# A decoder trunk in float32 pairs: four of eleven pairs of gate and up by seven products instead of eight

## The chip, the cores and the metric

The kernel runs on one core of one Trainium2 chip. The metric is the device time of one execution in microseconds (us). The engines are TensorE (PE, with its weight loads as PEld), VectorE (DVE), ScalarE (ACT), GpSimd (POOL) and SyncE (SP); transfers are issued from the queues of SP and Pool and carried by 16 DMA engines.

## The reference

Two decoder layers over x of 512 positions and 1024 features, float32. Each layer adds a token mixer and then a SwiGLU feed-forward part, each followed by a layer norm:

```python
def _swiglu(x, w_gate, w_up, w_down):
    return (jax.nn.silu(x @ w_gate) * (x @ w_up)) @ w_down

def reference(x, ...):
    for i in range(DEPTH):                       # DEPTH = 2
        h = _multiscale_pool(...) if i % 2 == 0 else _diff_attention(...)
        x = _layernorm(ALPHA * x + h, ln_mix_g[i], ln_mix_b[i])
        x = _layernorm(ALPHA * x + _swiglu(x, w_gate[i], w_up[i], w_down[i]), ln_ffn_g[i], ln_ffn_b[i])
    return x
```

The hidden width is 2816, that is 22 blocks of 128. Layer 0 mixes by pooling, layer 1 by attention.

## The kernel before

**Numbers.** Every float32 factor of a product is split into a high part (cast to the format that TensorE takes, on ACT) and a low part (value minus high part, on DVE). A product is three matmuls: high x high, high x low, low x high (`mm3`, lines 106 to 110).

**Weights.** All weights lie in one array `wall` of chunks of 128 x 1024. `fetch` loads a chunk from SP's queue into one of four buffers `raw`; `ready` casts it into `wh` (line 89) and makes `wl` (line 90), six buffers each.

**The feed-forward part, gate and up.** `ffn(layer, late)` treats the 22 blocks in the order 0, 11, 1, 12, and so on, so that block k and block k + 11 make pair k. For each block f, `product` runs 8 x 3 matmuls for gate and as many for up, with the weights stationary and x (`xt`, kept in two halves of 256 positions, high and low) moving, 512 columns at once. `gated` takes silu on ACT (line 459) and multiplies on DVE into `hid` (line 460). The first blocks (`early`: three in layer 0, two in layer 1) run first for the lower 256 positions and then for the upper 256, since x of the upper half comes late.

**The down product by seven products.** The product of `hid` with `w_down` is done by Strassen's scheme in Winograd's form: seven half-size products P1, Q5, P6, Q3, P7, P2, Q4 in place of eight. Its sums are made during gate and up. `sum_weights(k)` (lines 474 to 486) loads four blocks of the down weights from SP's queue (line 482), makes four sums on DVE (line 484) and stores them from Pool's queue into `tsum` in device memory (line 486); it runs eleven times a layer. `sum_hidden(k)` (lines 491 to 511) makes the sums of pair k of `hid`, keeps the high and low part of one quarter in `a11`, and stores the others, `v`, to `ssum` from Pool's queue (line 509). `items` is the list of down products; `prepare`, `split_item` and `left` get the factors of the next ones ready.

**Order.** Each engine and each queue carries out its instructions in the order in which the program issues them; the order is written out by hand, there is no planner. An instruction that waits holds what stands behind it on its engine or queue. `affine` (lines 188 ff.) applies a norm's scale and shift to `res`, two operations on DVE for each of four blocks of positions; before, it is called after the blocks that follow the early ones.

Of the kernel before, what the change touches and what calls it, by code (L numbers as in the profile page):

```python
# [12 lines left out]
F32 = mybir.dt.float32  # L13
# [32 lines left out]
DOWN = ("P1", "Q5", "P6", "Q3", "P7", "P2", "Q4")  # L46
PAIRS = [(0, 2), (2, 2), (4, 2), (6, 2), (8, 2), (10, 1)]
# [3 lines left out]
def trunk(ctx, tc, x, wall, pscale, lam_p, subln, table, lng, lnb, band, first, onehot, out):  # L51
# [85 lines left out]
    def load_gb(n):  # L137
        gb = keep.tile([P, 2, D], F32, tag="gb", name=f"gb{n}")
        nc.sync.dma_start(out=gb[:, 0, :], in_=lng[n : n + 1, :].broadcast_to([P, D]))
        nc.sync.dma_start(out=gb[:, 1, :], in_=lnb[n : n + 1, :].broadcast_to([P, D]))  # L140
        gbs[n] = gb
# [291 lines left out]

    ROWS = [slice(k, k + n) for k, n in PAIRS]

    def ffn(layer, late):
        n = 2 * layer + 1
        final = n == 2 * DEPTH - 1
        c0 = base[0]
        with tc.tile_pool(name=f"ffn{layer}", bufs=1) as fp:  # L440
# [5 lines left out]
            def product(acc, c, lo, hi):  # L446
                h, l = weights(c)
                for k in range(KB):
                    mm3(
                        wide(acc, lo, hi),  # L450
                        (h[:, k * P : (k + 1) * P], l[:, k * P : (k + 1) * P]),
                        x_at(k, lo, hi),
                        k == 0,
                        k == KB - 1,
                    )

            def gated(f, pg, pu):
                sg = keep.tile([P, S], F32, tag="y", name=f"sg{layer}_{f}", bufs=2)
                nc.scalar.activation(sg, pg, AF.Silu)  # L459
                nc.vector.tensor_tensor(hid[:, f, :], sg, pu, op=ALU.mult)  # L460

            c1 = c0 + 2 * FB
# [11 lines left out]
            def sum_weights(k):  # L474

                i, j = k // 2, k % 2
                c = slice(j * 512, (j + 1) * 512)
                b11, b12, b21, b22 = t = [
                    fp.tile([P, 512], F32, tag=f"b{b}", name=f"b{b}_{layer}_{k}") for b in range(4)
                ]  # L480
                for b in range(4):
                    nc.sync.dma_start(out=t[b], in_=block(i, b)[:, c])
                for z, x, y in ((b11, b11, b12), (b12, b12, b22), (b22, b11, b22), (b21, b22, b21)):
                    nc.vector.tensor_tensor(z, x, y, op=ALU.add)  # L484
                for m, z in enumerate((b11, b22, b12, b21)):
                    nc.gpsimd.dma_start(out=tsum[m, i, :, c], in_=z)

            late_low = []
            summed_rows = [0]

            def sum_hidden(k):
                first, second = hid[:, k, :256], hid[:, k, 256:]
                a12, a22 = hid[:, k + HALF, :256], hid[:, k + HALF, 256:]
                u = fp.tile([P, 2, 256], F32, tag="u", name=f"u{layer}_{k}", bufs=1)
                v = fp.tile([P, 2, 2, 256], F32R, tag="v", name=f"v{layer}_{k}", bufs=1)
                tt = nc.vector.tensor_tensor
                nc.scalar.copy(a11[:, 0, k, :], first)
                tt(second, second, a22, op=ALU.subtract)
                tt(a11[:, 1, k, :], first, a11[:, 0, k, :].bitcast(F32), op=ALU.subtract)
                tt(first, second, first, op=ALU.subtract)  # L500
                nc.vector.scalar_tensor_tensor(
                    u[:, 0, :], first, -1.0, a22, op0=ALU.mult, op1=ALU.subtract
                )
                tt(u[:, 1, :], a12, first, op=ALU.add)
                nc.scalar.copy(v[:, :, 0, :], u)  # L505

                def rest():
                    tt(v[:, :, 1, :], u, v[:, :, 0, :].bitcast(F32), op=ALU.subtract)
# [8 lines left out]
            early = 3 if layer == 0 else 2  # L517
            accs = [(bank(f"g{layer}_{f}"), bank(f"u{layer}_{f}")) for f in range(early)]
            for lo in (0, 256):
                for f in range(early):  # L520
                    for i in range(2):
                        product(accs[f][i], c0 + 2 * f + i, lo, lo + 256)
                        if not lo and (f, i) in late:
                            late[f, i]()
                        if not lo:
                            ready(c0 + 2 * early)
                    if lo:
                        ready(c0 + 2 * f + 6)
                        gated(order[f], *accs[f])
            sum_hidden(0)  # L530
            if layer:
                load_gb(n - 1)
# [570 lines left out]
```

## Time and profile before

| | |
|---|---|
| median of 3 runs | 981.76 us (979.96 to 982.25) |
| profiled execution | 983.17 us, its span 981.1 us |
| granted TensorE clock, mean | 0.995 |
| busy share: PE, DVE, ACT, POOL | 98%, 66%, 43%, 13% |
| moved by DMA | 188.59 MB, 192 GB/s in the mean |

The span runs from the first to the last instruction of the profiled execution. Busy times are unions of instruction spans, which for PE include the drain of one matmul under the next; the distance between the starts of two matmuls tells what one costs. In the rows of groups the count stands behind x, then the busy time and the mean of one in ns, then the idle time of the engine just before them and what ended it. In the rows of stretches the columns are the length, then each engine's busy time with its count, the granted clock, the share of the DMA engines and GB/s.

### The profile page before, as it was taken

The numbers are of one execution on the slowest core, as the hardware profiler recorded it, in microseconds if no ns is written. First come the engines' busy times: TensorE is split into PE (matmuls) and PEld (weight loads), VectorE is DVE, ScalarE is ACT, GpSimd is POOL, SyncE is SP. The second block draws the span as 40 slices with busy tenths as digits, with TensorE's granted clock in tenths as the row PEclk, the third lists the DMA queues.
The fourth block names the chain that finished last, engine by engine and source line by source line (L and its number), as shares of the span: only waits on it lengthen the run. The fifth ranks groups of instructions, "written<-read, shape, count | busy, mean of one in ns | idle before, by whom it ended". The sixth has DMA issues, their size and how long they took to land.

```text
span 981.1 us, 13416 instructions
## 1 busy us (share of the span) xinstructions
PE 963.2 (98%) x4974; PEld 820.6 (84%) x4974; DVE 643.4 (66%) x1007; ACT 420.5 (43%) x708; POOL 123.7 (13%) x195
## 2 busy tenths in 40 slices
PE   8999999999999999999999999999999999999995
PEld 8898888888888888988888888988888888888884
DVE  6845874455567577688777676756655555477687
ACT  5753222223326357656556554732223322244460
POOL 4201111111120211000000000011111111111102
PEclk9999999999999999999999999999999999999997
DMA  8247768655776984323222122276665566878942
GB/s 223 66 158 247 250 228 289 229 193 193 266 257 236 329 295 151 114 82 94 73 87 86 55 86 86 90 270 211 225 256 193 209 229 228 288 246 297 341 145 86
DMA packets 70079, 188.59 MB, mean 192 GB/s; under 512 B 15956, under 2 KB 16084, under 8 KB 70014
## 3 DMA queue, kind: packets, MB, share of 16 engines
q1 hardware_dynamic: 56588, 141.57, 42.1%
q0 software_dynamic: 13408, 46.15, 13.9%
q8 instruction: 39, 0.64, 0.3%
q14 instruction: 26, 0.21, 0.1%
q10 hardware_dynamic: 18, 0.02, 0.0%
HBM read 150.99 MB, written 36.72 MB: 191 GB/s over the span
## 4 chain that ended last, share of the span: by engine, by line
PE 94%; DVE 3%; ACT 1%; POOL 1%; issue 0%; POOLq 0%; DVEq 0%
PE P L629 13%; PE g L109 8%; PE u L108 8%; PE u L109 8%; PE g L108 8%; PE u L110 8%; PE g L110 8%; PE Q L629 6%; PE s L814 2%; PE v L108 2%; PE v L110 2%; PE v L109 2%; PE wo L108 2%; PE wo L109 2%; PE wo L110 2%; PE q L109 1%
## 5 line engine op out<-in xcount | busy, mean ns | idle before, releaser
L90 DVE TENSOR_TENSOR wl<-raw,wh 128x1024 fp32r<-128x1024 f32 x118 | 141.7, 1220 | 33.3 <-ACT wh L89 33.3
L89 ACT CAST wh<-raw 128x1024 fp32r<-128x1024 f32 x120 | 123.5, 1050 | 65.9 <-PE u L109 63.9
L109 PE MATMUL g<-xt,wh 128*128 128x512 f32 (+1 forms) x392 | 144.1, 368 | 0.5 <-DVE xt L90 0.5
L108 PE MATMUL g<-xt,wh 128*128 128x512 f32 (+1 forms) x392 | 144.3, 368 | 0.0
L108 PE MATMUL u<-xt,wh 128*128 128x512 f32 (+1 forms) x392 | 144.1, 368 | 0.0
L110 PE MATMUL u<-xt,wl 128*128 128x512 f32 (+1 forms) x392 | 144.0, 367 | 0.0
L109 PE MATMUL u<-xt,wh 128*128 128x512 f32 (+1 forms) x392 | 144.0, 367 | 0.0
L110 PE MATMUL g<-xt,wl 128*128 128x512 f32 (+1 forms) x392 | 144.0, 367 | 0.0
L460 DVE TENSOR_TENSOR hid<-sg,u 128x512 f32<-128x512 f32 x44 | 30.3, 688 | 154.9 <-PE u L110 154.5
L90 DVE TENSOR_TENSOR dl<-r,dh 128x1024 fp32r<-128x1024 f32 x84 | 94.3, 1132 | 38.8 <-ACT dh L89 38.7
L89 ACT CAST dh<-r 128x1024 fp32r<-128x1024 f32 x84 | 81.5, 979 | 69.6 <-PE P L629 31.7
L629 PE MATMUL P<-dh,xt 128*128 128x512 f32 x352 | 109.4, 390 | 0.0
L109 PEld LDWEIGHTS g<-xt,wh 128*128 128x128 f32 x392 | 73.9, 189 | 12.7 <-DVE xt L90 0.7
L110 PEld LDWEIGHTS u<-xt,wl 128*128 128x128 f32 x392 | 73.9, 189 | 12.3
L108 PEld LDWEIGHTS u<-xt,wh 128*128 128x128 f32 x392 | 73.9, 189 | 12.1
L110 PEld LDWEIGHTS g<-xt,wl 128*128 128x128 f32 x392 | 73.9, 188 | 12.2
L108 PEld LDWEIGHTS g<-xt,wh 128*128 128x128 f32 x392 | 73.9, 188 | 12.2
L109 PEld LDWEIGHTS u<-xt,wh 128*128 128x128 f32 x392 | 73.9, 188 | 12.0
L505 ACT CAST v<-u 128x512 fp32r<-128x512 f32 x22 | 13.7, 621 | 159.4 <-issue 142.5
L629 PEld LDWEIGHTS P<-dh,xt 128*128 128x128 f32 x352 | 66.1, 188 | 13.6
L484 DVE TENSOR_TENSOR b<-b,b 128x512 f32<-128x512 f32 x88 | 60.8, 691 | 18.4 <-DMA b<-in_wall 16.2
L459 ACT ACTIVATE sg<-g 128x512 f32<-128x512 f32 x44 | 26.3, 599 | 103.5 <-PE g L110 102.0
(189 smaller groups left out, 1792.5 us busy)
## 6 DMA issues: line engine op xcount, KB each, us to landing
raw<-in_wall SPq DMA_DIRECT2D x128, 512.0 KB, 4.2
b<-in_wall SPq DMA_DIRECT2D x88, 256.0 KB, 5.6
tsum<-b POOLq DMA_DIRECT2D x88, 256.0 KB, 4.7
r<-tsum SPq DMA_DIRECT2D x40, 512.0 KB, 4.7
r<-in_wall SPq DMA_DIRECT2D x30, 512.0 KB, 5.0
ssum<-v POOLq DMA_DIRECT2D x22, 512.0 KB, 4.0
xt<-ssum POOLq DMA_DIRECT2D x20, 512.0 KB, 6.0
res<-in_x SPq DMA_DIRECT2D x8, 256.0 KB, 6.4
```

The costliest lines, as they stand in the source:

```text
L89: nc.scalar.copy(dst_h, src)
L90: (low or nc.vector).tensor_tensor(dst_l, src, dst_h.bitcast(F32), op=ALU.subtract)
L108: nc.tensor.matmul(acc, ah, bh, start=start, stop=False)
L109: nc.tensor.matmul(acc, ah, bl, start=False, stop=False)
L110: nc.tensor.matmul(acc, al, bh, start=False, stop=stop)
L459: nc.scalar.activation(sg, pg, AF.Silu)
L460: nc.vector.tensor_tensor(hid[:, f, :], sg, pu, op=ALU.mult)
L484: nc.vector.tensor_tensor(z, x, y, op=ALU.add)
L505: nc.scalar.copy(v[:, :, 0, :], u)
L629: nc.tensor.matmul(accs[s], x[:, k, r], y[:, c], start=first and k == 0 and e == 0, stop=last and k == m - 1 and e == 2, skip_group_check= ...
L814: nc.tensor.matmul(accs[c][:, :wide], a[r, qs], b[r, :wide], start=i == 0, stop=i == 2)
```

## The change

**Split pairs.** Pairs 3, 5, 7 and 9 (`SPLIT`) of gate and up are done by the same seven products (`strassen`). The two-by-two blocks are the two halves of x's features against the two halves of positions, and gate and up of the pair. Each of the seven products is 2 x 4 x 3 matmuls of 256 columns, into three banks A, C and B. P1, P6, P7 and Q4 add up in A, Q5 and Q3 in C; after P1, Q5 and P6 ACT copies the bank out before the next product adds to it, after Q3, P7 and P2 DVE combines it with what was copied, and silu and the products of `gated` follow. The seven products need seven weight chunks made from four loaded ones: four sums on DVE (`sum` in `steps`).

**Sums of x.** `sums_of_x` makes the four sums of quarters of x that these products need, with their high and low parts, into `xs`, in steps between the products of the first blocks. `xs` later holds the left factors of the down product, in place of parts of `xt` and of `a11`, which is gone: P1's factors are split in `left`, and `left` makes P6's difference.

**Order of casts.** In `steps`, a chunk's cast comes ahead of the low part of the chunk before it. `advance` works these steps off; `refill` loads ahead as buffers come free.

**Down sums.** `load_terms(k + 1)` is issued a slot ahead of its use, from Pool's queue: four plain loads and, when the first two have landed, two loads that add to what is there (`accum_op`). `sum_terms(k)` makes the other two sums on DVE and stores all four. The buffers are rows of `hid` that are not yet in use, or the tile `gb`. For row 2 the sums stand ahead of the next load, since both use the same rows.

**Moved.** `affine` runs with blocks 0 to 3, three of them in the early stage of layer 0; the loads of `gb` are moved, in layer 1 to Pool's queue.

The diff, cut to its core:

```diff
+SPLIT = (3, 5, 7, 9)
+GATE = ("P1", "Q5", "P6", "Q3", "P7", "P2", "Q4")
...
-            a11 = fp.tile([P, 2, HALF, 256], F32R, name=f"a11_{layer}")
+            xs = fp.tile([P, 4, 2, 4, 256], F32R, name=f"xs{layer}")
...
+            def step(kind, j):
+                if kind == "cast" and steps and steps[-1][0] == "low":
+                    steps.insert(len(steps) - 1, (kind, j))
+                else:
+                    steps.append((kind, j))
...
+                    chunks += [(c, ()), (c, (c, c + 1)), (c, (c, c + 2)), (c + 2, ())]
+                    chunks += [(c + 1, (c + 1, c + 2)), (c + 3, ()), (c, (c, c + 3))]
+                    step("cast", j0)
+                    for w in (
+                        "low 0, sum 1, cast 1, sum 4, cast 3, cast 4, low 1, sum 2, cast 2, low 3, "
+                        "low 2, sum 6, cast 5, cast 6, low 4, low 5, low 6"
+                    ).split(", "):
+                        steps.append((w[:-2], j0 + int(w[-1])))
...
+            def load_terms(k):
+                ...
+                for q, b in enumerate((0, 1, 3, 2)):
+                    nc.gpsimd.dma_start(out=t[q], in_=block(i, b)[:, c])
+                for q, b in ((0, 1), (1, 3)):
+                    nc.gpsimd.dma_start(out=t[q], in_=block(i, b)[:, c], accum_op=ALU.add)
+                terms[k] = t
+
+            def sum_terms(k):
+                ...
+                t1, t3, b22, b21 = terms.pop(k)
+                tt(b22, t1, b22, op=ALU.add)                                   # line 648
+                tt(b21, b22, b21, op=ALU.add)
+                for m, z in enumerate((t1, b22, t3, b21)):
+                    nc.gpsimd.dma_start(out=tsum[m, i, :, c], in_=z)
+
+            def weight_sums():
+                k = summed_rows[0]
+                summed_rows[0] += 1
+                if k == 2:
+                    sum_terms(k)
+                if k + 1 < HALF:
+                    load_terms(k + 1)
+                if k != 2:
+                    sum_terms(k)
...
             def sum_hidden(k):
...
-                nc.scalar.copy(a11[:, 0, k, :], first)
-                tt(second, second, a22, op=ALU.subtract)
-                tt(a11[:, 1, k, :], first, a11[:, 0, k, :].bitcast(F32), op=ALU.subtract)
-                tt(first, second, first, op=ALU.subtract)
...
+                tt(u[:, 0, :], first, second, op=ALU.subtract)
+                tt(second, second, a22, op=ALU.subtract)
+                tt(u[:, 1, :], a12, first, op=ALU.subtract)
+                tt(u[:, 1, :], u[:, 1, :], second, op=ALU.add)
                 nc.scalar.copy(v[:, :, 0, :], u)
...
+            for lo in (0, 256):
+                for f in range(early):
+                    for i in range(2):
+                        product(accs[f][i], 2 * f + i, lo, lo + 256)
...
+                    if lo:
+                        advance(2 * f + 6)
+                        gated(order[f], *accs[f])
+                        affine(n - 1, f)
+                        weight_sums()
+                        if f < 2:
+                            next(sums)
+            sum_hidden(0)
...
+            def plain(f):
...
+                for i in range(2):
+                    product(a[i], j + i, 0, S)
+                    ahead(j + i + 5)
+                    if f >= 3:
+                        next(sums, None)
+                    if i == 0:
+                        settle()
+                gated(order[f], *a)
+                if f < SB:
+                    affine(n - 1, f)
+                if f in (2, 5, 8, 9, 12, 13, 16, 17, 20):
+                    weight_sums()
+                if f % 2:
+                    sum_hidden(k)
+
+            def strassen(k):
+                names = {"P1": "A", "P6": "A", "P7": "A", "Q4": "A", "Q5": "C", "Q3": "C", "P2": "B"}
...
+                for j, p in enumerate(GATE):
+                    acc = banks[names[p]]
+                    h, l = halves[index[k] + j]
+                    xh, xl = lefts[p]
+                    for f in range(2):
+                        o = acc[:, f * 256 : (f + 1) * 256]
+                        for kk in range(4):
+                            c = slice((4 * f + kk) * P, (4 * f + kk + 1) * P)
+                            for e, (w, x) in enumerate(((h, xh), (h, xl), (l, xh))):
+                                nc.tensor.matmul(o, w[:, c], x[:, kk, :], ...)      # line 794
+                    acc = both(acc)
+                    if p == "P1":
+                        g0 = tile_of(0)
+                        nc.scalar.copy(both(g0), acc)                            # line 803
+                    elif p == "Q5":
+                        nc.scalar.copy(second, acc)                              # line 805
+                    elif p == "P6":
+                        nc.scalar.copy(first, acc)                               # line 807
+                    elif p == "Q3":
+                        tt(first, acc, first, op=ALU.subtract)
+                    elif p == "P7":
+                        tt(second, second, acc, op=ALU.subtract)
+                    elif p == "P2":
+                        tt(both(g0), acc, both(g0), op=ALU.add)
+                        nc.scalar.activation(g0, g0, AF.Silu)
+                    else:
+                        g1 = tile_of(1)
+                        nc.scalar.activation(both(g1), acc, AF.Silu)
+                    ahead(index[k] + j + 6)
+                    if p == "P1":
+                        settle()
+                    elif p == "P2":
+                        tt(first, both(g0), first, op=ALU.mult)
+                    elif p == "Q4":
+                        tt(second, both(g1), second, op=ALU.mult)
+                sum_hidden(k)
```

More of the change, by code (lines that the diff above doesn't have):

```diff
@@ L476, in sum_weights @@
+            terms = {}
+            def load_terms(k):
                 i, j = k // 2, k % 2
                 c = slice(j * 512, (j + 1) * 512)
[L478 to L484, printed above, removed]
@@ L577, in prepare @@
                 while prepared[0] < min(upto, len(items)):
[L578 to L580 removed]
+                    refill()
                     split_item(prepared[0])
+                    held[0] -= 1
                     prepared[0] += 1
@@ L608, in ffn @@
+            f = early
+            while f < FB:
+                if f // 2 in SPLIT:
+                    strassen(f // 2)
+                    f += 2
+                else:
+                    plain(f)
+                    f += 1
+            load_gb(n)
             settle()
```

258 lines of the change are left out of this document (179 added, 79 removed).

## The prediction

> **What bounds the kernel now.** I read the page's busy shares first, then the chain that ended last, then the busy time by stage, then the timeline where the change acts.
>
> ```profile
> span 981.1 us, 13416 instructions
> ## 1 busy us (share of the span) xinstructions
> PE 963.2 (98%) x4974; PEld 820.6 (84%) x4974; DVE 643.4 (66%) x1007; ACT 420.5 (43%) x708; POOL 123.7 (13%) x195
> ...
> PE 94%; DVE 3%; ACT 1%; POOL 1%; issue 0%; POOLq 0%; DVEq 0%
> ```
>
> TensorE is busy for 98% of the span and carries 94% of the chain. A busy PE is no proof of a full PE, so the stages of layer 0 come next: the start of gate and up, the rest of it, and the down product.
>
> ```profile
> core 0: us, PE busy (x) PEld busy (x) DVE busy (x) ACT busy (x) POOL busy (x), PEclk, DMA share, GB/s
> 40.90:77.35 36.45, 36.44 (x304) 36.44 (x305) 18.02 (x22) 20.87 (x37) 2.24 (x4) 1.00 0.41 136
> 77.35:284.10 206.75, 206.75 (x913) 171.17 (x913) 119.91 (x168) 57.39 (x77) 29.35 (x52) 1.00 0.70 241
> 284.10:382.60 98.50, 98.50 (x435) 81.04 (x434) 73.48 (x94) 50.65 (x65) 13.38 (x20) 1.00 0.75 264
> ```
>
> In all three PE has no gap. So only less PE work can gain, and anything that makes PE wait is a loss at its full length. DVE has room: 18 of 36 us, 120 of 207, 73 of 98.5.
>
> **What PE saves.** A plain pair of gate and up (four chunks) issues 4 x 8 x 3 = 96 matmuls of 512 columns; a split pair issues 7 x 2 x 4 x 3 = 168 of 256 columns. The price is the step from one start to the next. The chain view gives 512 columns, PE's timeline in the half-width start of the same stage gives 256:
>
> ```profile
> 77.35 0.23 PE g L108
> ...
> 88.25 0.23 PE g L108
> ```
>
> ```profile
> 59.91 0.28 PE L108 MATMUL g<-xt,wh 128*128 128x256 f32 x1
> ...
> 62.78 0.28 PE L108 MATMUL u<-xt,wh 128*128 128x256 f32 x1
> ```
>
> 48 matmuls in 10.90 us are 0.2271 each, 24 in 2.87 us are 0.1196 each. So the half-width one costs 53%, not 50%, of a wide one. Plain: 96 x 0.2271 = 21.80 us. Split: 168 x 0.1196 = 20.09 us. The saving is 1.71 us a pair, not an eighth of 21.8 (2.7), and 13.7 us for eight pairs (four in each of two layers). That is the ceiling of the change.
>
> The Trainium skill ("TensorE: Matmul & The Clock Gate", Back-to-back issue gap) gives the isolated gap as N/2.4 + 2.5 ns, 215.8 and 109.2 for these widths; by it the saving would be 2.4 us a pair, 19 us in all. The rows above differ from it, and they decide.
>
> **What DVE and ACT get.** Prices of the pieces, on their engines:
>
> ```profile
> L90 DVE TENSOR_TENSOR wl<-raw,wh 128x1024 fp32r<-128x1024 f32 x118 | 141.7, 1220 | 33.3 <-ACT wh L89 33.3
> L89 ACT CAST wh<-raw 128x1024 fp32r<-128x1024 f32 x120 | 123.5, 1050 | 65.9 <-PE u L109 63.9 <-issue 1.3 <-ACT line L422 0.7
> ```
>
> ```profile
> 197.88 0.42 DVE L498 TENSOR_TENSOR hid<-hid 128x256 f32<-128x256 f32 x1
> 198.22 0.42 DVE L499 TENSOR_TENSOR a<-hid,a 128x256 fp32r<-128x256 f32 x1
> 198.68 0.42 DVE L500 TENSOR_TENSOR hid<-hid 128x256 f32<-128x256 f32 x1
> ...
> 201.58 1.22 DVE L90 TENSOR_TENSOR wl<-raw,wh 128x1024 fp32r<-128x1024 f32 x1 [1.68 <-ACT wh L89]
> 202.72 0.69 DVE L508 TENSOR_TENSOR v<-u,v 128x512 fp32r<-128x512 f32 x1
> 203.32 2.87 DVE L484 TENSOR_TENSOR b<-b,b 128x512 f32<-128x512 f32 x4
> 206.10 1.22 DVE L90 TENSOR_TENSOR wl<-raw,wh 128x1024 fp32r<-128x1024 f32 x1
> ```
>
> ```profile
> 102.44 1.22 DVE L189 TENSOR_TENSOR res<-res,gb 128x1024 f32<-128x1024 f32 x1
> ...
> 103.69 1.23 DVE L190 TENSOR_TENSOR res<-res,gb 128x1024 f32<-128x1024 f32 x1
> ```
>
> From start to start a 1024-wide operation costs 1.14 us when the next is independent and 1.25 when it depends; 512-wide 0.60 and 0.70; 256-wide 0.34 and 0.46.
>
> Steady state (a split pair and the plain pair beside it, 20.1 + 21.8 = 41.9 us of PE): 11 low parts and 4 weight sums, 15 x 1.14 = 17.1; 13 operations of 512 (five bank readings and products of the split pair, two gated, two low parts of v, four of the down sums) x 0.65 = 8.5; eight of 256 in `sum_hidden` x 0.40 = 3.2. That is 28.8 us of 41.9, with six buffers of lookahead: hidden. ACT gets 11 casts and nine 512-wide, 11 x 1.05 + 9 x 0.62 = 17.1: hidden. The one tight spot is that P6 adds to the bank of P1, so ACT must copy P1 out during Q5 (2.87 us), and that copy stands in ACT's queue behind the cast of `v`, which waits for `sum_hidden` of the pair before. In steady state gated, two down sums and `sum_hidden` end 3.6 us after the plain pair (0.1 + 0.6 + 0.7 + 0.6 + 1.6); cast and copy make that 5.0; P6 is due at 2 x 2.87 = 5.7. It holds, by 0.7 us.
>
> The start of layer 0 is different. `affine`, three down sums, four sums of x, four differences of x and four low parts of x are all queued between the first gated product and the first split pair. Count of DVE's queue from the end of the first `u` (62.78 + 2.87 = 65.65) up to `sum_hidden(2)`: 33 operations of 1024 (8 affine, 4 + 4 + 4 for x, 10 low parts, 3 sums), six followed by a dependent one: 27 x 1.14 + 6 x 1.25 = 38.3; 16 of 512 (6 gated, 8 down sums, 2 low parts of v): 12 x 0.60 + 4 x 0.70 = 10.0; 12 of 256: 6 x 0.34 + 6 x 0.46 = 4.8. Sum 53.1, with 0.1 at its start 53.2. Then on ACT:
>
> ```profile
> 199.97 0.62 ACT L505 CAST v<-u 128x512 fp32r<-128x512 f32 x1 [7.37 <-issue]
> ```
>
> Cast of v and copy of P1, taken at 0.62 each, with hand-overs: 54.5. PE is due at P6 after two half-width f (2 x 5.74), three wide f (3 x 10.90) and P1 and Q5 (2 x 2.87): 49.9. So PE waits 4.6 us, at about 115.6 us of the span. The other products are covered (low part of chunk 14 at 47.6, last x part at 49.9).
>
> In layer 1 only two f are early, so a fourth wide f takes the place of a half-width one: P6 is due 5.2 us later, at 55.1, for the same DVE work. I take 0.3 us there.
>
> A wait of 4.6 us also cools the clock. After PE's last work, and in the first stage, the trace shows:
>
> ```profile
> 970.00:971.00 1.00, 0.00 (x0) 0.00 (x0) 1.00 (x3) 0.00 (x0) 0.00 (x0) 0.98 0.00 0
> 971.00:972.00 1.00, 0.00 (x0) 0.00 (x0) 0.97 (x3) 0.00 (x0) 0.00 (x0) 0.50 0.80 295
> ```
>
> ```profile
> 7.55 0.58 PE L311 MATMUL pool<-fh,xt 128*128 128x256 f32 x1 [1.01 <-ACT fh L89]
> ...
> 18.43 0.38 PE L316 MATMUL pool<-bh,xt 128*128 128x256 f32 x1
> 18.64 0.28 PE L325 MATMUL pool<-bh,xt 128*128 128x256 f32 x1
> ```
>
> PE's last matmul was over before 969 and the clock is at half by 971, so 4.6 us is enough to lose it. Cold steps are 0.21 (18.43 to 18.64) against 0.12, so cold time loses 44%. Between nothing and the 11.1 us that the first stage stayed cold (4.9 us lost), I take 5 us, 2.2 lost, because that first stage had gaps and this one is dense.
>
> The Trainium skill (same page, Part 1: The HAM clock gate) says that an idle window of about 3.4 us halves the clock and a busy one of that length restores it. By it the loss would be 1.5, the sum 0.7 lower; the trace agrees that it drops within about 2 us of idling.
>
> **DMA.** The down sums' terms leave SP for Pool's queue, and two of four additions become accumulating loads:
>
> ```profile
> b<-in_wall SPq DMA_DIRECT2D x88, 256.0 KB, 5.6
> tsum<-b POOLq DMA_DIRECT2D x88, 256.0 KB, 4.7
> ...
> ssum<-v POOLq DMA_DIRECT2D x22, 512.0 KB, 4.0
> ```
>
> ```profile
> L486 POOL DMA_DIRECT2D tsum<-b x88 | 48.3, 555 | 37.2 <-DVE b L484 35.5 <-DVE wl L90 1.4 <-issue 0.2
> ```
>
> Bytes: 2 x 256 KB more for each of 11 rows, 5.8 MB on 49.8 (241 GB/s x 206.75): about 274 GB/s, share near 0.80, where the down product ran at 264 and 0.75 without a PE gap. Pool issues 11 transfers a row at about 0.6 us: 7 us of 21. An accumulating load waits for the plain load beneath it and holds Pool's queue, where the stores of the row before and `ssum` stand behind it. No trace shows an accumulating load; from below I price it as a plain one (5.6), from above at twice that. At 5.6: in a plain pair the odd row's load is issued at about 5, lands at 10.8, is accumulated by 16.6 and is wanted at 22.5 (21.8 + 0.7); even rows have longer. At the start of layer 0, row 0's sums end 4.4 after the first `u`; row 2's load is issued at 5.7, lands at 11.3, its accumulation at 16.9; DVE's count wants it at 18.6. Nothing, in both. The last place is pair 9, whose result rows are the buffer of row 9's sums. Counted from the start of f=16: row 8's sums end at 12.9 (10.9 + 0.1 + 0.6 + 1.3), its stores land at 17.7, row 10's load at 23.3, and only behind its accumulations are row 9's stores issued, by 25.1, to land at 29.8. Q5 ends at 2 x 10.9 + 5.7 = 27.5, a cast puts its copy at 28.6, Q3 is due at 30.4, and a copy from 29.8 ends there: 0.3 us a layer, 0.6 in all (0 to 3 each).
>
> In the down product P1's factors are now split there, six times cast 0.62 and low part 0.60, and P6 subtracts first: per item 1.14 + 0.60 + 0.65 = 2.4 us of DVE under 12 x 0.2271 = 2.7 of PE. Hidden. Casts ahead of low parts only move ACT's work earlier: nothing.
>
> **Sum.** 13.7 - 4.6 - 2.2 - 0.3 - 0.6 = 6.0 us less. The profiled execution took 983.17 (span 981.1, 2.1 around it) and would take 977.2. The median of the runs is 981.76, 1.4 below the profiled one; so I predict 975.8.
>
> **Rivals.** (1) All is covered: DVE's start turns out some 10% shorter, or the copy of P1 isn't late. The wait and the cold time go: 981.76 - 13.7 + 0.9 = 969.0. For it: DVE's count has a margin that a tenth of 53 would close. Against: every price is from back-to-back rows. Chance 0.13. Further on the same side, 0.02: the half-width step comes out at half of the wide one, 0.1136, so that a pair saves 21.80 - 19.08 = 2.72 and the sum is 8.1 lower, 967.7; the 24 steps above speak against it. The isolated gap of the Trainium skill, cited above, is this case.
>
> (2) Loads are not early. In layer 0 six landings stand in series on Pool's queue (store of row 0, load, accumulation, store of row 2, load 3, `ssum` of pair 0), and the cast of v for pair 1 waits for the last. At the medians: store issued 4.5, landed 9.2, load 14.8, accumulation 20.4, store 25.1, load 30.7, `ssum` issued 31.3 and landed 35.3; wanted at 37 by DVE's count. One us more each makes it 41.3, DVE loses about 5, and PE with it; with 0.7 us more for each pair 9, 975.8 + 5 + 1.4 = 982.2: no change. For it: the DMA share rises. Chance 0.15.
>
> (3) Slower: the accumulating load is the bound. It is issued 11 us before DVE needs it on odd rows and 7 before row 2. From a landing of about 11 us on, DVE's down sum, `sum_hidden`, the cast of v and the copy of P1 slip together and P6 waits in pairs 5, 7 and 9 of both layers. At 13 us: six waits of 2, some 6 more at the first rows: 975.8 + 18 = 993.8; it is slower than now from about 11.3. For it: reading and writing back the target may double a load. Against: 5.6 must double. Chance 0.22.
>
> **How the numbers follow.** My forecast has 0.48 (972 to 979 for a wait between 2 and 8 us with its cold time). Range 969.5 to 986: it leaves out the lower half of rival 1 and the worst of rival 3. A run of this kernel can be told from no change at about 0.3%, 2.9 us. Faster: 0.48 + 0.15 less the edge: 0.62. Same 0.15, slower 0.23.
>
> **What would show it.** Right: matmuls of line 794 start 0.12 us apart; one PE gap of about 4.6 us before P6 of layer 0's first split pair, ended by ACT's line 803, with a dip of the clock; none in steady state. Wrong: DVE idle behind accumulating loads (line 648 waiting for DMA), PE gaps in pairs 5, 7 and 9, or steps other than 0.12.

## The result, and the profile after

The changed kernel takes 1005.42 us (median of 6 runs, 1003.14 to 1008.11) against 981.9 for the kernel before, run beside it (median of 6): 1.0243 times as long, 95% interval 1.0221 to 1.0264. I had forecast 975.8 and a range that ended at 986.0. The sign was wrong. The profiled execution took 1004.16.

The page of the changed kernel, its head and its chain:

```profile
span 1002.4 us, 14587 instructions
## 1 busy us (share of the span) xinstructions
PE 959.1 (96%) x5550; PEld 842.0 (84%) x5550; DVE 725.5 (72%) x1069; ACT 463.5 (46%) x754; POOL 213.9 (21%) x329
...
PEclk9999899999799999999999999999799999999999
...
PE 19%; issue 3%; DMA 3%; DVE 3%; POOL 1%; ACT 0%; POOLq 0%; DVEq 0%; ACTq 0%
```

TensorE is still busy for 96%. The page follows the chain back only to about 692 us, so its 19% can't be set against the 94% before; the part that it follows runs through DMA, DVE and Pool as well as PE. The granted clock dips in three slices. Where the time went is read from four stretches, first of the kernel before, then of the changed one: gate and up of layer 0 from the first wide block on, the down product of layer 0 up to attention, and the same two of layer 1, the last up to the end of the span.

```profile
77.19:283.94 206.75, 206.75 (x915) 171.17 (x913) 119.75 (x168) 57.39 (x77) 29.23 (x51) 1.00 0.70 241
283.94:392.26 108.32, 108.07 (x487) 89.01 (x486) 80.17 (x103) 59.66 (x86) 14.75 (x22) 1.00 0.72 250
645.92:863.56 217.64, 217.64 (x963) 180.19 (x962) 122.96 (x171) 60.08 (x80) 29.26 (x52) 1.00 0.68 238
863.56:981.10 117.54, 105.28 (x463) 86.58 (x461) 85.72 (x113) 48.21 (x63) 17.55 (x24) 0.96 0.63 222
```

```profile
73.86:297.12 223.26, 205.24 (x1203) 183.92 (x1202) 153.02 (x188) 78.54 (x100) 62.28 (x100) 0.95 0.73 228
297.12:407.37 110.25, 110.14 (x488) 89.38 (x486) 82.53 (x108) 60.07 (x88) 13.18 (x19) 1.00 0.69 242
661.02:885.06 224.04, 214.04 (x1250) 191.06 (x1249) 159.12 (x194) 80.42 (x101) 65.97 (x108) 0.98 0.76 237
885.06:1002.40 117.34, 107.52 (x463) 86.87 (x461) 88.59 (x118) 49.00 (x65) 16.14 (x21) 0.98 0.62 220
```

Gate and up became 16.5 and 6.4 us longer, 22.9 together, instead of 14 shorter; layer 0's down product 1.9 longer; the last stretch 0.2 shorter. The first wide block began 3.3 earlier (73.86 against 77.19), because the first stage left its half clock sooner in this execution. That stage's code is not changed, and kernels that share it begin the first wide block anywhere from 73.6 to 77.3 (the last section). Sum 21.3, the difference of the spans. In gate and up PE is idle for 18.0 and 10.0 us, where it had no gap before. The waits of PE name two places:

```profile
PE A L794 <- ACT sg L803: 18.0, 2, 10.1
PE C L794 <- ACT hid L805: 9.9, 2, 7.8
```

The first is P6 of pair 3, once a layer (10.1 in layer 0, 7.9 in layer 1); the second is Q3 of pair 9 (7.8 and 2.1).

### The profile page after: what moved, and what is told of

It reads as the page before. It is cut to its first block, busy times and chain, and to the rows that moved or that the text cites. A ratio compares the mean times of both kernels' runs of the same rounds, so it can differ in the third digit from the quotient of the medians.

```text
span 1002.4 us, 14587 instructions
## 1 busy us (share of the span) xinstructions
PE 959.1 (96%) x5550; PEld 842.0 (84%) x5550; DVE 725.5 (72%) x1069; ACT 463.5 (46%) x754; POOL 213.9 (21%) x329
## 5 line engine op out<-in xcount | busy, mean ns | idle before, releaser
L549 ACT CAST gh<-raw 128x1024 fp32r<-128x1024 f32 x104 | 107.0, 1050 | 113.8 <-PE g L111 32.5
L552 DVE TENSOR_TENSOR gl<-raw,gh 128x1024 fp32r<-128x1024 f32 x104 | 125.3, 1220 | 22.5 <-ACT gh L549 22.3
L858 PE MATMUL P<-dh,xs 128*128 128x512 f32 x440 | 139.4, 395 | 0.0
L858 PEld LDWEIGHTS P<-dh,xs 128*128 128x128 f32 x440 | 82.9, 188 | 19.2
L858 PE MATMUL P<-dl,xs 128*128 128x512 f32 x220 | 86.8, 395 | 0.0
L110 PE MATMUL g<-xt,gh 128*128 128x512 f32 (+1 forms) x200 | 76.2, 381 | 0.0
L111 PE MATMUL g<-xt,gh 128*128 128x512 f32 (+1 forms) x200 | 76.2, 381 | 0.0
L112 PE MATMUL u<-xt,gl 128*128 128x512 f32 (+1 forms) x200 | 76.1, 381 | 0.0
L112 PE MATMUL g<-xt,gl 128*128 128x512 f32 (+1 forms) x200 | 76.1, 381 | 0.0
L110 PE MATMUL u<-xt,gh 128*128 128x512 f32 (+1 forms) x200 | 76.1, 381 | 0.0
L111 PE MATMUL u<-xt,gh 128*128 128x512 f32 (+1 forms) x200 | 76.1, 381 | 0.0
L676 ACT CAST v<-u 128x512 fp32r<-128x512 f32 x22 | 13.7, 621 | 130.7 <-issue 65.3
L92 DVE TENSOR_TENSOR wl<-raw,wh 128x1024 fp32r<-128x1024 f32 x38 | 46.1, 1221 | 9.4 <-ACT wh L91 9.3
```

What stands on the lines that cost most here:

```text
L92: (low or nc.vector).tensor_tensor(dst_l, src, dst_h.bitcast(F32), op=ALU.subtract)
L110: nc.tensor.matmul(acc, ah, bh, start=start, stop=False)
L111: nc.tensor.matmul(acc, ah, bl, start=False, stop=False)
L112: nc.tensor.matmul(acc, al, bh, start=False, stop=stop)
L549: nc.scalar.copy(halves[j][0], t)
L552: tt(l, t, h.bitcast(F32), op=ALU.subtract)
```

## The experiments

My theory (A) was that these two waits, with the half clock behind them, are the loss, and that each has its own cause: a backlog at the start of the stage, and the order of Pool's queue at pair 9. The rival (B) was that the new down sums, or DVE with them, hold every split pair. Two smaller questions were the slower down product and the way in which the backlog reaches PE. All kernels are the changed one with the edits shown.

**No split pair.**

```diff
-SPLIT = (3, 5, 7, 9)
+SPLIT = ()
```

> No pair is split; the early loads, the accumulating loads, the sums of x, the moved affine and the place of the down factors stay. My theory (A): the loss of the changed kernel is two waits that only split pairs have, P6 of each layer's first split pair (18.0 us in its trace, about 5 more of half clock) and Q3 of pair 9 (9.9), and a slower step of the down product (0.2324 for 0.2267 us, 66 matmuls in 12 phases, 4.5). Without split pairs the waits and the gain (14.3 by the trace) both go: 1005.4 - 33.1 + 14.3 = 986.6, about 4.5 above the kernel before, no PE wait in gate and up. Rival (B): the accumulating loads and their traffic hold gate and up whatever the pairs do: PE waits stay at lines 110 to 112 and the time stays above 995.

Measured 981.99, ratio 1.0006 (0.9994 to 1.0018): no wait in gate and up, which takes what it took before (206.75 and 217.64), in the same two stretches of this kernel's trace:

```profile
74.33:281.08 206.75, 206.75 (x914) 171.18 (x913) 112.36 (x148) 60.33 (x76) 62.18 (x100) 1.00 0.77 248
644.97:862.60 217.63, 217.63 (x962) 180.19 (x961) 118.14 (x154) 61.50 (x77) 65.26 (x106) 1.00 0.75 244
```

B falls; early loads, accumulating loads, the sums of x and the moved `affine` cost TensorE nothing there by themselves. That it came out as the kernel before and not 4.5 slower is told below, with the factors.

**First split pair later.**

```diff
-SPLIT = (3, 5, 7, 9)
+SPLIT = (5, 7, 9)
```

> Pairs 5, 7 and 9 are split, pair 3 is not. A: the wait at P6 belongs to the backlog of the start, and 42 us later it is worked off: 18.0 and about 5 us of half clock go, two savings of 1.8 are given up: 1005.4 - 23 + 3.6 = 986. B (a split pair asks for more of DVE or of Pool's queue than there is): P6 of pair 5 waits in its place, some 8 us a layer, 1005 or more.

Measured 991.99 (984.45 to 996.33), ratio 1.0088 (1.0048 to 1.0128). P6 waits nowhere any more, so its wait did belong to the start. The profiled execution, at the median, missed A's 986 because the other wait was longer in it, as the row below shows. Three of the seven runs lie between 984.5 and 986.0 and four between 992.0 and 996.3; with one trace it isn't shown that Q3's wait parts them.

```profile
PE C L794 <- ACT hid L805: 14.5, 2, 11.1
```

**Row 9's stores first.**

```diff
-                if k == 2:
+                if k in (2, 9):
                     sum_terms(k)
                 if k + 1 < HALF:
                     load_terms(k + 1)
-                if k != 2:
+                if k not in (2, 9):
```

> Row 9 of the down sums is added and stored ahead of the loads of row 10 on Pool's queue, as row 2 is. A: Q3 of pair 9 waits because the stores stand behind row 10's accumulating loads; the wait (9.9 in two layers) falls below 1 us: 1005.4 - 9.5 = 996. B (the transfers themselves are slow here, whatever their order): the stores land hardly earlier, the wait stays above 5 us, 1001 to 1005.

Measured 988.61, ratio 1.0071 (1.0053 to 1.0090): 16.8 us less than the changed kernel, more than the 9.5 expected, since the half clock behind the wait goes too: in the two profiled executions gate and up is 15.9 shorter, 11.0 of it waits and 4.9 PE's busy time for the same matmuls. Q3's wait is gone from the list; P6 still waits 17.0. The cause is seen in the changed kernel's trace at pair 9 of layer 0, in Pool's timeline, ACT's and PE's:

```profile
237.06 2.49 POOL L651 DMA_DIRECT2D tsum<-b  x4
245.80 2.14 POOL L639 DMA_DIRECT2D b<-in_wall  x4 [6.25 <-DMA tsum<-b]
249.38 1.78 POOL L641 DMA_DIRECT2D b<-in_wall  x2 [1.44 <-DMA b<-in_wall]
250.60 2.75 POOL L651 DMA_DIRECT2D tsum<-hid  x4
...
260.54 0.59 ACT L805 COPY hid<-C 128x512 f32<-128x512 f32 x1 [8.95 <-DMA tsum<-hid]
...
261.18 0.80 PE L794 MATMUL C<-xs,gh 128*128 128x256 f32 x2 [7.81 <-ACT hid L805]
```

Row 8's stores go out, row 10's loads wait for them to land (both use the tile `gb`), the accumulating loads wait for the plain ones, and only then are row 9's four stores issued; they land at 260.5. Q5's copy goes into the row that they are read from.

**Both together.** `SPLIT = (5, 7, 9)` and row 9's stores first.

> Pairs 5, 7 and 9 are split and row 9's stores come first: both waits are avoided. A: no wait above 1 us in gate and up; six savings of 1.8 (10.7) less 1.7 for the slower down product: 981.4 - 9.0 = 972.4. B (the accumulating loads or DVE hold every split pair): P6 waits in pairs 5, 7 or 9, 980 or more.

Measured 970.83, ratio 0.9891 (0.9866 to 0.9917): no wait in gate and up, and faster than the kernel before. Gate and up is 10.2 us shorter in both layers together (201.79 and 212.45), 1.7 for each of six split pairs. A's two places account for the loss.

**Row 2 in rows of its own.** On top of row 9's stores first; the plain order of `weight_sums` again for k = 2.

```diff
+                elif k == 2:
+                    t = [hid[:, row, :] for row in (3, 14, 8, 19)]
```

> On top of row 9's stores first (988.6), row 2 of the down sums is loaded into rows 3, 14, 8 and 19 of hid, which are free, and no longer into row 0's rows; its loads need not wait until row 0's stores have landed, and row 1's stores do not stand behind that wait. A: DVE's waits for these landings at the start (lines 648 and 591; 3.2 us in layer 0 and 4.2 in layer 1 with row 9 first) are part of P6's wait (17.0): it falls to about 9.6, and 1.5 of half clock with it: 979.7. B (P6's wait is the backlog of DVE's and ACT's own work alone, the landings are hidden in it): the wait stays at 17, 988.

Measured 987.7, ratio 1.0053 (1.0032 to 1.0073), not to be told from 988.61 by the runs; in the traces gate and up is 2.8 us shorter (428.6 against 431.4). The wait of P6 fell from 17.0 to 12.7, not to 9.6: in layer 0 DVE's waits for landings are gone (P6 waits 7.0 in place of 10.4), in layer 1 one stays, 3.4 us, for row 1's stores (5.7 in place of 6.6). A's direction holds, its size was half wrong.

**ACT's order.** Twice I moved the cast of v on ACT, with row 9's stores first: once behind P1's copy, once behind P7's part, by taking the cast into `rest`, and the second time by calling `settle` later as well.

```diff
-                nc.scalar.copy(v[:, :, 0, :], u)
                 def rest():
+                    nc.scalar.copy(v[:, :, 0, :], u)
...
-                    if p == "P1":
+                    if p == "P7":          # second kernel only
                         settle()
```

> On top of row 9's stores first (988.6), the cast of v moves on ACT from the end of sum_hidden to the place where its low part is made, which in a split pair is behind the copy of P1. A: DVE's backlog reaches PE only because that copy stands behind the cast of v on ACT; without it P6 waits for the low part of the second sum of x (line 597), 4.4 us in layer 0 and 2.5 in layer 1 by the trace of the changed kernel, in place of 17.0: 976.5. B (the backlog is late for PE anyway, in the low parts of the chunks): the waits move to P7, P2 and Q4 and stay above 14 in sum: 986 or more.

> As the run with the copy first, but the cast of v now stands behind P7's part of the split pair, so that the copies of P1, Q5 and P6 all stand ahead of it on ACT. A: DVE's backlog reaches PE through this one place in ACT's queue; P6 then waits only for the low part of the second sum of x (3.3 us in layer 0, 2.0 in layer 1, by the run with the copy first) and P7 some 2 us for a low part behind sum_hidden: sum about 8 in place of 17.0, from 988.6 to 978. B (the backlog is late for PE in any order): sum 12 or more, 984 or more.

Measured 988.24 (ratio 1.0061, 1.0041 to 1.0082) and 988.99 (1.0080, 1.0059 to 1.0102): no gain over 988.61, and A fell on this point. P6 waits less, but Q3 waits now, for Q5's copy: the waits sum to 12.0 and 12.8 in place of 17.0, PE is busy 3.5 and 4.1 us longer in gate and up for the same matmuls, and the two stretches together come to 429.9 and 431.3, against 431.4 with row 9's stores first alone. ACT's timeline of the second kernel, and DVE's:

```profile
127.11 1.04 ACT L549 CAST gh<-raw 128x1024 fp32r<-128x1024 f32 x1 [6.30 <-DVE raw L543]
128.06 0.58 ACT L804 COPY hid<-C 128x512 f32<-128x512 f32 x1
```

```profile
125.51 0.42 DVE L675 TENSOR_TENSOR u<-u,hid 128x256 f32<-128x256 f32 x1
125.86 1.22 DVE L543 TENSOR_TENSOR raw<-raw,raw 128x1024 f32<-128x1024 f32 x1
```

A cast of a summed chunk stands ahead of the copy, and its sum (line 543) stands behind `sum_hidden` on DVE. The backlog is late for PE in either order; the order only decides which instruction passes it on.

**Even pairs.** The first split pair starts a plain pair later, and pair 9 isn't split; row 9's stores come first.

```diff
-SPLIT = (3, 5, 7, 9)
+SPLIT = (4, 6, 8, 10)
...
-                if f in (2, 5, 8, 9, 12, 13, 16, 17, 20):
+                if f in (2, 4, 6, 7, 10, 11, 14, 15, 18):
                     weight_sums()
```

> Pairs 4, 6, 8 and 10 are split, row 9's stores come first, and the down sums are made behind blocks 2, 4, 6, 7, 10, 11, 14, 15 and 18. The first split pair starts 22 us later than pair 3 does, so the start's backlog (P6 waited 10.4 and 6.6 us with row 9 first) is worked off in time, and pair 9, whose rows hold terms, is not split. A: no wait above 1 us in gate and up, two savings of 1.8 more than with pairs 5, 7 and 9 (970.8): 967.2. B: pair 10 is late, since P1's factors are split beside its seven chunks, or P6 of pair 4 waits: 971 or more.

Measured 971.67 (968.86 to 977.24), ratio 0.9903 (0.9880 to 0.9925). One wait of 1.5 us at P6 of pair 4 is left. The time can't be told from that of pairs 5, 7 and 9, and A's 967.2 was not reached; in the traces gate and up is 1.7 us shorter than there (412.5 against 414.2), where A had 3.6.

**The same without accumulating loads.**

```diff
-                for q, b in ((0, 1), (1, 3)):
-                    nc.gpsimd.dma_start(out=t[q], in_=block(i, b)[:, c], accum_op=ALU.add)
...
+                tt(t1, t1, t3, op=ALU.add)
+                tt(t3, t3, b22, op=ALU.add)
                 tt(b22, t1, b22, op=ALU.add)
```

> As the run with even pairs, without accumulating loads: four plain loads a row and four sums on DVE, 1.3 us more of DVE and 512 KB less traffic a row. If the accumulating loads cost nothing on the path once the order on Pool's queue is right: within 1 us of the run with even pairs. If they are a burden (issue of 0.88 us against 0.55, a landing more in the chain): faster by over 1 us. If DVE is too full for the sums: slower by over 1 us, P6 waiting.

Measured 983.38, ratio 1.0012 (1.0000 to 1.0025): 11.7 us more than with them, all of it in gate and up (424.2 against 412.5 in the traces). P6 waits in six of the eight split pairs: 5.8 us at pair 4 of layer 0, 1.0 at pair 4 of layer 1, and 0.67 or 0.68 at pairs 6 and 8 of both:

```profile
PE A L794 <- ACT sg L803: 9.5, 6, 5.8
...
185.23 0.50 PE L794 MATMUL A<-xs,gh 128*128 128x256 f32 x2 [0.67 <-ACT sg L803]
```

The accumulating loads are what makes room for the split pairs on DVE. With 1.3 us more of DVE ahead of P6, P6 waits 0.67, so the steady state's margin is 0.6; I had put it at 0.7.

**Where the down factors lie.** Three runs: factors from Q5 on back in `xt` (on the changed kernel), `xs` allocated ahead of `hid` (with row 9's stores first), and the high and low parts of `xs` 16 KB apart (with pairs 5, 7, 9 and row 9's stores first).

```diff
-                o = 2 * (j % 2)                                  # first
-                t = xs[:, j // 2 % 4, :, o : o + m, :]
+                if p == "P1":
+                    o = 2 * (j % 2)
+                    t = xs[:, j // 2 % 4, :, o : o + m, :]
+                else:
+                    o = 2 * (j % 4)
+                    t = xt[:, (1 + j // 4) % 2 if final else 1, :, o : o + m, :]
...
-            xs = fp.tile([P, 4, 2, 4, 256], F32R, name=f"xs{layer}")
+            xs = fp.tile([P, 2, 4, 4, 256], F32R, name=f"xs{layer}").rearrange("p i m k t -> p m i k t")   # third
```

> The left factors of the down product from Q5 on are made in xt again, as in the kernel before; P1's stay in xs. A: the step of a down matmul hangs on the tile that its stationary operand is read from: 0.2267 from xt, 0.2324 from xs. 12 of 14 phases go from 15.33 to 14.96: 1005.4 - 4.5 = 1001. B (the step comes from the work beside it, P1's factors on ACT and DVE or the traffic): the phases stay at 15.33 and the time at 1005.

> On top of row 9's stores first (988.6), xs is allocated ahead of hid, so that it lies at another address; nothing else changes. If the step of the down matmuls hangs on the address of the stationary operand, the phases of 66 matmuls leave 15.33 us (14.96 if it is as from xt): 986.5, since only layer 0's 1.9 us lengthened the span. If it hangs on the tile's use or form, they stay at 15.33: 988.6.

> Pairs 5, 7 and 9 split and row 9's stores first (970.8), with the high and low parts of xs 16 KB apart in a partition in place of 4 KB. If the longer step of the down matmuls (15.33 us for 66) comes from how close the parts of the stationary operand lie, it falls towards 14.96 (in xt they lie 8 KB apart) and the time to about 969; if not, 15.33 and 970.8.

Groups of down matmuls in the kernel with factors in `xt`, then in the changed kernel (the last number but one is the mean of one in ns):

```profile
L862 PE MATMUL P<-dh,xt 128*128 128x512 f32 x352 | 109.9, 390 | 2.5 <-DMA xt<-ssum 2.5
L862 PE MATMUL P<-dh,xs 128*128 128x512 f32 x88 | 27.9, 395 | 0.0
```

```profile
L858 PE MATMUL P<-dh,xs 128*128 128x512 f32 x440 | 139.4, 395 | 0.0
```

The slower step follows the tile within one kernel: 66 matmuls take 14.96 us from `xt` and 15.33 from `xs`. But the time did not follow: 1006.53 (998.91 to 1011.47), ratio 1.0246 (1.0194 to 1.0298). In layer 0, where `xt` has four slots for factors and `xs` eight, loads of factors from `ssum` came late (2.5 and 0.8 us of waits), so that the down product from its first to its last matmul took 110.8 there against 108.9; in layer 1 it took 104.9 against 107.1. Beside a spread of 12.6 us over its four runs neither shows in the time. The other address and the other distance of the parts changed nothing: 991.43 (ratio 1.0087, 1.0060 to 1.0113) and 972.33 (0.9905, 0.9891 to 0.9920), the phases at 15.34 in both. Only one other place in the same pool was tried. What makes `xs` slower stays open.

**Mended versions.** Even pairs with factors in `xt` where slots suffice; the change's own pairs with all of the above; even pairs with the cast of v behind P7's part and layer 1's factors from Q5 on in `xt`.

> As the run with even pairs, and the left factors of the down product lie in xt again where there are slots enough: in layer 1 from Q5 on, in layer 0 for Q5, P6, P2 and Q4, while Q3 and P7, which are loaded, stay in xs with its eight slots. A: layer 0 saves 4 x 0.37 = 1.5 us, layer 1 the 1.8 by which the run with factors in xt was shorter from P1 to the end: 3.3 below the run with even pairs. B: loads of factors come late again, 2 us a layer as in the run with all factors in xt: no gain.

> The change's own pairs 3, 5, 7 and 9 with all that the runs showed mended: row 9's stores first, row 2 in rows of its own, the cast of v behind P7's part, layer 1's down factors from Q5 on in xt. By A the waits at the start fall to some 4 us in both layers together: 981.4 - 14.3 + 0.1 (layer 0's slower down product less layer 1's tail) + 4 = 971. By B they stay above 10: 978 or more.

> Even pairs with the cast of v behind P7's part and layer 1's down factors from Q5 on in xt, layer 0's all in xs. By A no wait is left in gate and up (0.5 to 1.5 us at pair 4 with even pairs before) and none for factors in layer 0's down product (1.1 with factors in xt there): 1 us below the run with even pairs and factors in xt, 969 to 970. By B: no change.

Measured 971.27 (ratio 0.9881, 0.9863 to 0.9899), 982.66 (1.0013, 0.9997 to 1.0029) and 968.72 (0.9863, 0.9844 to 0.9882). The first did not gain the 3.3 us: layer 1 came out 2.2 shorter in its down product, layer 0 waited 1.1 for a factor. In the second, pair 3 still comes too early, as in every order tried: Q3 waits 8.7 and P6 3.7 us, and the saving is used up. The third is the best version that I found, 1.4% faster than the kernel before, and its gate and up has no gap, at full clock (the first two rows; the third is layer 1's down product up to the end of the span):

```profile
77.14:276.95 199.81, 199.81 (x1202) 179.15 (x1201) 150.79 (x186) 77.66 (x99) 62.33 (x100) 1.00 0.77 252
...
640.83:851.52 210.69, 210.69 (x1251) 188.16 (x1249) 156.57 (x192) 79.15 (x100) 66.27 (x108) 1.00 0.77 248
851.52:967.00 115.48, 105.29 (x464) 86.59 (x462) 89.94 (x121) 49.61 (x67) 16.14 (x21) 0.97 0.66 232
```

## Why the prediction was wrong, point by point

The terms of the sum, forecast and then measured in the traces: saving 13.7 and 13.9 (this in the best version, without waits); waits at P6 of the first split pairs 4.9 and 18.0; waits at Q3 of pair 9 0.6 and 9.9; half clock 2.2 and 8.8; slower down product, not in the sum, 1.7 net. The two steps that failed are the ones that priced Pool's loads and stores: "Nothing, in both" at the start, and 0.3 us a layer at pair 9. The half clock is their consequence, and was too small on its own as well. Two of the signs that were named for being wrong came: line 648 waiting for DMA, once, and PE gaps in pair 9.

**The saving was right.** Where no wait disturbs it, gate and up is 6.94 and 6.95 us shorter (206.75 to 199.81, 217.64 to 210.69): 1.74 a pair, forecast 1.71. A stretch is PE's busy time and its waits, so the sum of gate and up in the changed kernel closes: 13.9 saved, 28.0 of waits, and PE busy 5.4 and 3.4 us longer than in the best version for the same matmuls (205.24 against 199.81, 214.04 against 210.69): 28.0 + 8.8 - 13.9 = 22.9. That the 8.8 are half clock is read from the granted clock, below. So the forecast had the gain and priced 7.7 of losses, where there were 36.8.

**The wait at the start: place and mechanism right, size wrong.** P6 of layer 0's first split pair waits for line 803, as forecast, 10.1 us in place of 4.6; layer 1, forecast at 0.3, waits 7.9. The count of DVE's work was good: in the kernel with row 2 in its own rows, DVE runs from the first gated product at 66.03 to the end of `sum_hidden(2)` at 121.54 in layer 0, 55.5 us with 2.1 of waits, so 53.4 of work against the 53.1 that I counted. What failed is the step that put the loads at "Nothing, in both". DVE's waits in this stretch of the changed kernel, layer 0 and then layer 1:

```profile
88.24 2.36 DVE L591 TENSOR_TENSOR hid<-xt 128x1024 f32<-128x1024 f32 x2 [3.05 <-DMA tsum<-hid]
96.35 0.69 DVE L578 TENSOR_TENSOR hid<-sg,u 128x512 f32<-128x512 f32 x1 [1.61 <-ACT sg L577]
111.31 0.69 DVE L578 TENSOR_TENSOR hid<-sg,u 128x512 f32<-128x512 f32 x1 [0.48 <-ACT sg L577]
```

```profile
673.48 0.69 DVE L578 TENSOR_TENSOR hid<-sg,u 128x512 f32<-128x512 f32 x1 [0.21 <-ACT sg L577]
681.37 0.69 DVE L648 TENSOR_TENSOR hid<-hid 128x512 f32<-128x512 f32 x1 [4.81 <-DMA hid<-in_wall]
684.61 2.36 DVE L591 TENSOR_TENSOR hid<-xt 128x1024 f32<-128x1024 f32 x2 [0.68 <-DMA tsum<-hid]
692.11 0.69 DVE L578 TENSOR_TENSOR hid<-sg,u 128x512 f32<-128x512 f32 x1 [1.61 <-ACT sg L577]
707.08 0.69 DVE L578 TENSOR_TENSOR hid<-sg,u 128x512 f32<-128x512 f32 x1 [0.48 <-ACT sg L577]
```

5.1 and 7.8 us; added to the forecast waits they make 9.7 and 8.1, measured 10.1 and 7.9. Of them 3.1 (layer 0) and 5.5 (layer 1) are waits for landings, the rest is for silu. Three links were missing. Row 2's loads use row 0's rows and wait for row 0's stores (the chain of rival 2, which I had written out and given 0.15). The sums of x use rows 4, 5, 15 and 16, in which row 1's terms lie until their stores have landed, and those stand behind row 2's accumulating loads; this reuse I had not seen. And the silu of a plain block stands on ACT behind the high parts of the sums of x, 2.1 to 2.3 us, where I had let the gated product follow at once. The run with row 2 in its own rows bears out the landings: it lost the 3.2 us of them that layer 0 still had with row 9's stores first, and P6 waited 3.4 less there. No run moved the silu, so its share is read from the trace alone.

**Pair 9: the chain was right, its landings too short.** Counted from the start of block 16 (222.85), I had row 10's load at 17.7 and row 9's stores landed at 29.8, with Q3 due at 30.4. Q3 was due at 30.5; the load was issued at 23.0 and the stores had landed at 37.7. I had taken 4.7 for a store of sums, the median before. In this traffic the median is 6.5 for those out of `hid` and 4.4 for those out of `gb`, but here Pool waited 6.25 for the last of row 8's, which come out of `gb`, and row 9's, all issued by 30.5, took another 7.2. The wait is not a fixed price: with the same order on Pool's queue Q3 waited 7.8 and 2.1 in this trace (layer 0, layer 1), 11.1 and 3.4 with pairs 5, 7 and 9, and 1.5 and 7.7 with factors in `xt`. The mean of 0.73 to 0.76 of the DMA engines, which I had forecast as 0.80, says nothing of this: while PE waited, they were at 0.99 (the first of the two stretches, its last columns are clock, share and GB/s).

```profile
253.37:261.18 7.81, 0.00 (x0) 0.00 (x0) 0.29 (x1) 0.64 (x2) 0.72 (x1) 0.72 0.99 325
261.18:268.00 6.82, 6.82 (x35) 6.82 (x36) 2.46 (x3) 3.37 (x4) 0.00 (x0) 0.57 0.50 196
```

**The half clock: right in kind, too small.** Three waits lost the clock, not one, and each lost about 3 us (8.8 in three), not 2.2. The second row above shows one: after the wait PE ran 6.82 us at a mean clock of 0.57, a loss of 2.9. The stretches behind the two waits of P6 show the others, 2.2 and 3.1 by the same reckoning:

```profile
122.55:130.00 7.45, 7.45 (x46) 7.45 (x47) 5.05 (x5) 4.81 (x6) 0.72 (x1) 0.70 0.73 253
718.33:726.00 7.67, 7.67 (x41) 7.67 (x42) 5.04 (x5) 4.80 (x6) 0.72 (x1) 0.60 0.70 208
```

Behind the fourth wait, the 2.1 us at Q3 in layer 1, the granted clock stayed at 1.00. The Trainium skill ("TensorE: Matmul & The Clock Gate", Part 1: The HAM clock gate) gives at least one window of about 3.4 us for either turn; by one window, as an estimate, each wait would have lost 1.7, 5.1 in all. The measured loss is larger, and the rows decide.

**The down product.** "Hidden" looked only at DVE's work and had no term for PE's step; this cost 1.7 us net. That the step follows the stationary operand's tile stood in the profile before, in two groups that I did not compare:

```profile
L629 PE MATMUL P<-dh,xt 128*128 128x512 f32 x352 | 109.4, 390 | 0.0
...
L629 PE MATMUL P<-dh,a 128*128 128x512 f32 x88 | 27.9, 395 | 0.0
```

The change puts all factors where only P1's were slow. Layer 0 pays 1.9 us. Layer 1 pays as much, up to DVE's last operation, which ends 112.35 us after the stretch began before the change and 114.21 after it:

```profile
974.49 1.42 DVE L181 SCALAR_TENSOR_TENSOR res<-res,rs,gb 128x512 f32<-128x512 f32 x2 [0.45 <-POOL rs L161]
```

```profile
997.86 1.41 DVE L183 SCALAR_TENSOR_TENSOR res<-res,rs,gb 128x512 f32<-128x512 f32 x2 [0.46 <-POOL rs L163]
```

But from there to the end of the span it is 5.2 us before and 3.1 in the changed kernel and all its versions, which nearly hides it (117.54 against 117.34); with factors in `xt` the stretch is 115.5. No run shows why the end is shorter. So the kernel without split pairs came out even and not 4.5 slower.

**The rivals.** (3) had the wrong mechanism: an accumulating load lands like a plain one (median 4.9 against 5.2 us, the rows are below), and DVE isn't held by it in steady state. (2) had the right chain on Pool's queue and the wrong price, 982.2: DVE waited for row 1's stores and row 2's load and not for `ssum`, and the rival left out the half clock and took the landings near the medians of before. (1), all covered, is what the mended even pairs reach: 968.7 against the 969.0 worked out there. That they agree so closely is partly luck, since layer 0's slower down product and the shorter end are not in that sum.

## What to carry to other kernels

A gain of 14 us that comes in pieces of 1.7 is lost in one wait: before such a change, follow for every buffer that is used twice who reads it last, and how many landings stand in series on the queue of the one who must free it. Take landings at the traffic that the change makes, in the stretch where they matter, not at the median of the profile before. When a backlog is the cause, try the new work one plain pair later first: here it mended all but 1.5 us at once, while changing the order of the instructions behind it only moved the wait.

## What the runs showed of the hardware that I had not expected

Accumulating loads (line 641) cost Pool more to issue, 0.88 us against 0.55 to 0.63, but land no later. Each pair of rows is the group and the time to landing, of line 641 and of line 639:

```profile
L641 POOL DMA_DIRECT2D hid<-in_wall x28: 849/882/1184, 51.7 to 832.0; - x28
...
DMA to landing us min/median/max: 3.9/4.9/9.4
```

```profile
L639 POOL DMA_DIRECT2D hid<-in_wall x56: 538/625/886, 44.2 to 827.6; - x56
...
DMA to landing us min/median/max: 2.9/5.2/9.7
```

The Trainium skill ("DMA: Bandwidth & Descriptors", SWDGE vs HWDGE vs iDMA) says that only GpSimd can issue an accumulating transfer; so the loads could not leave Pool's queue, and no run here tried it.

A down matmul of 512 columns takes 0.2267 us with its stationary operand in `xt` and 0.2324 in `xs` or `a11`, at both places and both spacings of `xs` that were tried.

The first stage, the same in all kernels, went from the slow steps to the fast ones at 18.6 us in the profiled execution before and at 11.1 in that of the changed kernel, where a 512-wide step falls from 0.58 to 0.24 us in the rows below. The first wide block began 3.3 us apart in the two; with row 9's stores first it began at 73.6, and in the same kernel with `xs` ahead at 77.3. That this is the clock is taken from the steps alone: the granted clock of the rows reads 1.00 in this stage throughout.

```profile
10.47 0.74 PE L305 MATMUL sc<-sch,one 1*128 1x512 f32 x1
11.05 0.39 PE L306 MATMUL sc<-scl,one 1*128 1x512 f32 x1
11.29 0.39 PE L305 MATMUL sc<-sch,one 1*128 1x512 f32 x1
```
